# A two-layer streaming encoder: spatial mixing for eight feature tiles at once, first parts for the down projections in mid-group, parked sums in two steps a group

## The chip, the cores and the metric

The kernel runs on one core of one Trainium2 chip. The metric is device time in microseconds from launch to end; lower is better. Engines are named as in the profile: PE (matmul) with its weight loads (PEld), DVE (vector), ACT (scalar and activation), POOL and SP (here they only issue DMAs; POOL also makes a few constants).

## The reference

Two layers over 256 positions of 2048 features, all in fp32. Layer 0 mixes tokens with a gMLP spatial gating unit, layer 1 with latent attention; each mixer is followed by a gated MLP with a causal width-3 convolution, and each sub-layer ends in a layer norm of `ALPHA * x + sublayer(x)`. The parts that the change touches:

```python
def gmlp_mixer(x, w_in, ln_g, ln_b, w_s, b_s, w_out):
    z = jax.nn.gelu(x @ w_in)                       # 2048 -> 2 x 6144
    u, v = jnp.split(z, 2, axis=-1)
    v = layer_norm(v, ln_g, ln_b)
    v = v.reshape(B, S // 128, 128, 8, 768)         # windows of 128 positions, 8 groups of features
    w = w_s * mask[None]                            # chunk-causal, 128 x 128 for each group
    s = jnp.einsum('gij,bnjgd->bnigd', w, v) + jnp.transpose(b_s)[None, None, :, :, None]
    return (u * s.reshape(B, S, HALF)) @ w_out      # 6144 -> 2048

def conv_ffn(x, w_up, conv_w, conv_b, w_down):
    h = conv(x @ w_up) + conv_b                     # 2048 -> 2 x 5504, causal, width 3, per feature
    a, g = jnp.split(h, 2, axis=-1)
    return (jax.nn.silu(g) * a) @ w_down            # 5504 -> 2048
```

## The kernel before

Every weight passes through the core once, in chunks of 128 x 2048 fp32 (1 MB). SP loads a chunk into one of three `raw` buffers. ACT casts it to a high part (`wh`, line 127), DVE subtracts to a low part (`wl`, line 130). A product is made of high times high, high times low and low times high, all through the helper `mm`, so nearly every matmul has line 234. `Feed` keeps the order of the chunks: `feed.next()` hands out the next one, and casts and loads some chunks ahead, into 14 slots of one size with the tag `big`. Those slots also hold the activations. A second tag, `side`, has six slots.

Order: first the v half of the gMLP (six slices), then the u half, then the gMLP's down projection ("wo"), the first gated MLP ("up", then "dn"), attention, and the second gated MLP. A scheduler orders the instructions of each engine from the program order, its own estimates, and the order that is fixed by `keep_in_program_order` (`pin`).

The u half has 12 groups (`gi`) of four feature tiles. A group accumulates four PSUM banks over four chunks, in a wide pass (moving 512 columns) and a narrow one (256) for each chunk; the order of the two alternates, so that a group begins and ends with 16 wide matmuls. Eight banks exist in the pool. After a group, `gate` treats its tiles one after the other: ACT copies one half of the bank (`lo_u`, line 388), DVE adds the other (`h_u`, line 390), ACT applies GELU (line 788), PE mixes positions with the group's 128 x 128 weights (`s`: two matmuls a tile, two records each), DVE makes a bias (`sb`, line 793), scales the mixed values (`sg`, line 798, two operations of 128 columns) and multiplies (`pT`, line 800).

An up projection has 21 groups of up to four banks (two tiles of `a`, two of `g`). Group 1 to 20 have four chunks, group 21 has two. After a group, `pair` runs the convolutions and the gate on ACT and DVE (lines 388, 390, 835 to 853).

Some down chunks are of the kind "seven": beside the parts of the weights they need parts of sums of weights. For eight chunks per gated MLP these parts are made during the up projection and parked in HBM ("parked"; `park`, lines 150 to 181). A piece goes in steps: POOL's queue loads the chunk (`praw`, line 164); ACT casts, DVE subtracts, POOL stores two parts (`pwh`, `pwl`); DVE makes four additions in place (line 154); ACT casts, DVE subtracts, POOL stores the parts of the sums (`pth`, `ptl`). `next(jobs, None)` runs one step, behind every chunk from group 2 on; the steps of a piece are six, two of them empty. Later the parts are fetched back from HBM to the `side` slots.

`acts.make` makes the high and low parts of the activations of one unit (two tiles) of a down projection: unit 0 and 2 of "dn" are wide (a cast and a low part), unit 1 is parked and needs four subtractions (`turn`, lines 290 to 293) and two casts with their low parts. Units 0 and 1 are made after group 19, unit 2 after group 20.

The places in the code that set this order:

```python
for f in range(4): gate(4 * gi + f, acc[f])        # u half, after each group
if gi > 1: next(jobs, None)                        # up projection, behind each chunk
if gi == 19: acts.make(units 0 and 1)              # up projection, after the group
if gi == 20: acts.make(unit 2)
```

Of the kernel before, what the change touches and what calls it, by code (L numbers as in the profile page):

```python
# [15 lines left out]
P = 128  # L16
S = 256
# [43 lines left out]
        NF_FF: ("0e 1p 2e 3s 4e 5e 6p 7e 8s 9e 10e 11p 12e 13s 14e 15p 16e 17s 18e 19s 20e 21e",  # L61
                "21e 20e 19p 18e 17s 16e 15p 14e 13s 12e 11p 10s 9e 8s 7p 6e 5s 4e 3e 2e 1e 0e")}
KINDS = {"e": "wide", "s": "seven", "p": "parked"}
LEAD = 5
KEEP = {"wide": 4, "seven": 6, "parked": 6}

# [6 lines left out]
class Feed:  # L73
# [76 lines left out]
    def park(self, i):  # L150

        nc, pin = self.nc, self.pin
        tile = lambda n, dt: self.pool.tile([P, 2048], dt, tag="side", name=f"{n}{i}", bufs=SLOTS["side"])
        add = lambda o, a, b: pin(nc.vector.tensor_tensor(o, a, b, ALU.add))
        self.kept[i] = kept = {}

        def store(n, t, cols):
            d = self.dram.tile([P, cols], F32, tag=f"kept{n}{i}", name=f"kept{n}{i}", bufs=1)
            pin(nc.gpsimd.dma_start(d, t[:, 0:cols].bitcast(F32)))
            kept[n] = d  # L160

        ap = self.chunks[i][0]
        raw = tile("praw", F32)
        pin(nc.gpsimd.dma_start(raw.rearrange("p (k c) -> p k c", k=ap.shape[1]), ap))
        yield
        yield
        yield
        for n, o, cols in (("w", 512, 1536), ("t", 0, 2048)):
            hi, lo = tile(f"p{n}h", F32R), tile(f"p{n}l", F32R)
            pin(nc.scalar.copy(hi[:, 0:cols], raw[:, o : o + cols]))  # L170
            pin(nc.vector.tensor_tensor(lo[:, 0:cols], raw[:, o : o + cols], hi[:, 0:cols].bitcast(F32), ALU.subtract))  # L171
            store(f"{n}h", hi, cols)
            store(f"{n}l", lo, cols)
            if n == "w":
                yield
                r = [raw[:, 512 * i : 512 * (i + 1)] for i in range(4)]
                add(r[1], r[1], r[0])
                add(r[0], r[0], r[2])
                add(r[2], r[2], r[1])
                add(r[3], r[3], r[2])  # L180
                yield
# [32 lines left out]
def trunk(ctx: ExitStack, tc: tile.TileContext, x, xT, gm_in, gm_wout, ffn_up, ffn_dn,  # L214
# [12 lines left out]
    def slot(shape, name, dt=F32, tag="big"):  # L227
        return big.tile(shape, dt, tag=tag, name=name, bufs=SLOTS[tag])

    def bank(name):  # L230
        return ps.tile([P, 512], F32, tag="bank", name=name)
# [154 lines left out]
    def sum_halves(acc, name):  # L386
        lo = tp.tile([P, S], F32, tag="t1", name=f"lo_{name}", bufs=T1)
        nc.scalar.copy(lo, acc[:, S : 2 * S])
        h = tp.tile([P, S], F32, tag="t1", name=f"h_{name}", bufs=T1)
        nc.vector.tensor_tensor(h, acc[:, 0:S], lo, ALU.add)  # L390
        return h
# [90 lines left out]
    def down(n_k, src, tag, ln, acts, skew=SKEW):  # L482

        ln.begin()
        seq = plan(n_k)
        line = seq[0] + seq[1]
        late, at = [], 0
        fetched = max([i for i, t in enumerate(line) if t[1] == "parked"], default=len(line))
        for hf, units in enumerate(seq):
            n = len(units)  # L490
            last = [u for u, kind in units if kind != "wide"][-1]
            acc = Banks(f"{tag}{hf}", OWN + DIRECT if hf else DIRECT + OWN)
            for i, (u, kind) in enumerate(units):
                left = n - 1 - i if hf == 1 else n
                for n2, v2 in enumerate(line[at : at + 3]):
                    acts.make(*v2, "side" if at + n2 > fetched or at + n2 >= len(seq[0]) and v2[1] == "parked" else "big")
                if i == n - 8:
                    ln.fetch(hf)
                got = feed.next(splits=2 if left > 5 or left == 0 else 3, loads=2 if left > 2 or left == 0 else 1)
                if left == 6:  # L500
                    ln.prep()
                a, sums = acts.got[u]
                if left < skew:
                    late.append((a, *got))
                elif kind == "wide":
                    acc.eight(a, *got)
                else:
                    acc.seven(a, sums, *got, 512 if kind == "parked" else 0)
                    if u == last:
                        for j, t in enumerate(acc.rest()):  # L510
                            ln.fold(j // 2, 2 * hf + j % 2, t)
                at += 1
                for v2 in [v2 for v2 in acts.got if not any(v2 == w2 and n2 < KEEP[kind2]
                                                            for n2, (w2, kind2) in enumerate(line[at:]))]:
                    acts.got.pop(v2)
            if hf == 0:
                for j, m in enumerate(DIRECT):
                    ln.piece(j // 2, j % 2, acc.acc[m])

        def end(b, f):  # L520
            for i, (a, hi, lo) in enumerate(late):
                for j in range(len(a[b])):
                    prod_b([acc.acc[DIRECT[2 * b + f - 2]]], a[b][j], hi, lo, [(j * 1024 + (f - 2) * 512, 512)],
                           False, i == len(late) - 1 and j == len(a[b]) - 1)

        return [[None, None] + [acc.acc[DIRECT[2 * b + f]] for f in range(2)] for b in range(2)], end
# [251 lines left out]
    pT = [None] * 6  # L778
    acts = Acts(pT, "wo", NF_GM)

    def gate(F, acc):
        g = F // 6
        sl, pos = F // 8, F % 8
        if pT[sl] is None:
            pT[sl] = slot([P, 8, S], f"pT{sl}", tag="side" if sl else "big")
        h = sum_halves(acc, f"u{F}")
        u = tp.tile([P, S], F32, tag="t1", name=f"u{F}", bufs=T1)
        nc.scalar.activation(u, h, AF.Gelu_apprx_tanh)
        sp = bank(f"s{F}")
        for b in range(2):  # L790
            mm(sp[:, b * P : (b + 1) * P], v[sl][:, b, pos * P : (pos + 1) * P], wTg[:, g, :], True, True)
        t = tp.tile([P, P], F32, tag="sbias", name=f"sb{F}", bufs=1)
        nc.vector.scalar_tensor_tensor(t, rowsum[:, g, :], cst[:, C_GMB + F : C_GMB + F + 1], bsb[:, g, :],
                                       ALU.mult, ALU.add)
        s = tp.tile([P, S], F32, tag="t1", name=f"sg{F}", bufs=T1)
        for b in range(2):
            c = slice(b * P, (b + 1) * P)
            nc.vector.scalar_tensor_tensor(s[:, c], sp[:, c], cst[:, C_GMG + F : C_GMG + F + 1], t,
                                           ALU.mult, ALU.add)
        nc.vector.tensor_tensor(pT[sl][:, pos, :], u, s, ALU.mult)  # L800

    def park_all(until):

# [5 lines left out]
    for gi in range(12):  # L809
        acc = [bank(f"u{gi}_{f}") for f in range(4)]  # L810
        for c in range(4):
            hi, lo = feed.next()
            prod_a(acc, xhl, range(4 * c, 4 * c + 4), hi, lo)
            if gi > 0:
                next(jobs, None)
            if gi % 2 == 0 and gi < 10 and c in (1, 2):
                norm_v(gi // 2 + 1, c - 1)
        if gi == 11:
            for t in plan(NF_GM)[0][:2]:
                acts.make(*t)  # L820
        for f in range(4):
            gate(4 * gi + f, acc[f])
        if gi == 10:
            acts.make(*plan(NF_GM)[0][2])

# [16 lines left out]
    def ffn(layer, ln, acc, end, last):  # L842
# [28 lines left out]
        for gi in range(1, 22):  # L871
            nt, nk = (4, 4) if gi < 21 else (2, 8)
            acc = [bank(f"up{layer}_{gi}_{f}") for f in range(nt)]
            for c in range(KD // nk):
                hi, lo = feed.next()
                prod_a(acc, xhl, range(nk * c, nk * c + nk), hi, lo)
                if gi > 1:
                    next(jobs, None)
                if gi == 1 and c == 0:
                    after(1, 1, None)  # L880
                    for f in range(2):
                        pair(f, hb[0][:, f * S : (f + 1) * S], hb[1][:, f * S : (f + 1) * S])
            for f in range(nt // 2):
                pair(2 * gi + f, acc[f], acc[nt // 2 + f])
            if 1 < gi < 6:
                old.restore(gi - 2)
            if gi in (4, 6):
                old.park(gi // 2 - 2)
            if gi == 19:
                for t in plan(NF_FF)[0][:2]:  # L890
                    acts.make(*t)
            if gi == 20:
                acts.make(*plan(NF_FF)[0][2])
        ln = Norm(2 * layer + 1, {}, old.put_away, last)
        return (ln, *down(NF_FF, act, f"dn{layer}", ln, acts, 4 if last else SKEW))

# [379 lines left out]
```

## Time and profile before

| | |
|---|---|
| runs shown | 2482.6, 2479.5, 2482.21 us |
| median | 2482.21 us |
| the profiled execution | 2481.38 us |
| its span, first to last instruction | 2479.3 us |
| granted TensorE clock | 0.999 |
| u half of the gMLP, on PE | from 256.2 us to 547 us |
| first up projection | from 821 us to 1283 us |
| second up projection | from 1789 us to 2247 us |

All times inside an execution are microseconds from the start of the span. A row of a timeline has the start, the length, the engine, the line, the operation, the tiles written and read, the shape, the count of instructions merged in it and, in brackets, the idle time before it with what ended that. A row of the groups has the count, busy us, mean ns of one, and the idle time before them by what ended it. A row of the waits has who waited for whom, then us in total, times and the longest. Matmuls are pipelined, so the length of one is more than the distance to the next. A stall of PE is therefore read from the starts.

### The profile page before, as it was taken

What the parts mean: (1) busy time and instruction counts of PE and PEld (TensorE: products, weight loads), DVE (VectorE), ACT (ScalarE), POOL (GpSimd) and SP (SyncE); (2) the same over time, 40 slices, a digit from 0 to 9 for tenths busy, and PEclk for the clock granted to TensorE, in tenths of its full rate; (3) what the DMA queues carried; (4) which work ended last, traced back from release to release, by engine and by line L of the source; (5) the groups of instructions that cost most, each with busy time, mean ns of one, the idle gap of its engine ahead of it and who ended that gap; (6) DMA issues with size and microseconds to landing.
All of it is one profiled execution on the core that took longest, in us unless ns stands there. A gap on an engine that the chain in (4) does not pass through costs nothing. (4 is left out here: it accounts for less than half of the span.)

```text
span 2479.3 us, 33472 instructions
## 1 busy us (share of the span) xinstructions
PE 2463.7 (99%) x12947; PEld 2117.2 (85%) x12947; DVE 1999.7 (81%) x2834; ACT 1428.6 (58%) x1995; POOL 88.4 (4%) x171
## 2 busy tenths in 40 slices
PE   9999999999999999999999999999999999999998
PEld 7888888888888888888888888988888888888886
DVE  7999866679898788787677897867598778768798
ACT  6666544456565756566554466565566656555453
POOL 0000000000000000000000000000000000000000
PEclk9999999999999999999999999999999999999999
DMA  7556544556665689788558885544488789647885
GB/s 280 204 206 220 202 170 170 182 175 216 209 204 204 216 349 342 298 323 325 182 199 327 301 295 191 189 157 161 171 307 331 292 331 352 233 153 287 298 326 201
DMA packets 108992, 606.16 MB, mean 244 GB/s; under 512 B 10273, under 2 KB 11041, under 8 KB 61601
## 3 DMA queue, kind: packets, MB, share of 16 engines
q1 hardware_dynamic: 84832, 463.51, 52.6%
q0 software_dynamic: 24000, 140.52, 14.8%
q8 instruction: 101, 1.65, 0.3%
q14 instruction: 59, 0.48, 0.1%
HBM read 538.98 MB, written 65.01 MB: 244 GB/s over the span
## 5 line engine op out<-in xcount | busy, mean ns | idle before, releaser
L130 DVE TENSOR_TENSOR wl<-raw,wh 128x1024 fp32r<-128x1024 f32 (+4 forms) x693 | 968.7, 1419 | 214.2 <-ACT wh L127 130.7
L127 ACT CAST wh<-raw 128x1024 fp32r<-128x1024 f32 (+4 forms) x693 | 820.3, 1211 | 387.5 <-PE u L234 84.6
L234 PE MATMUL up<-xhl,wh 128*128 128x512 f32 x2624 | 612.0, 390 | 0.9 <-ACT wh L127 0.9
L234 PEld LDWEIGHTS up<-xhl,wh 128*128 128x128 f32 x2624 | 487.2, 188 | 99.5 <-ACT wh L127 1.8
L234 PEld LDWEIGHTS up<-xhl,wl 128*128 128x128 f32 x2624 | 325.9, 192 | 8.4 <-DVE wl L130 2.1
L234 PE MATMUL up<-xhl,wl 128*128 128x256 f32 x2624 | 328.9, 283 | 1.4 <-DVE wl L130 1.4
L234 PE MATMUL u<-xhl,wh 128*128 128x512 f32 x768 | 184.7, 393 | 0.1
L234 PEld LDWEIGHTS u<-xhl,wh 128*128 128x128 f32 x768 | 141.1, 188 | 31.5 <-issue 3.7
L127 ACT CAST th<-ts 128x1536 fp32r<-128x1536 f32 x106 | 110.1, 1051 | 85.1 <-DVE ts L137 59.4
L130 DVE TENSOR_TENSOR tl<-ts,th 128x1536 fp32r<-128x1536 f32 x106 | 125.4, 1218 | 8.0 <-PE dn_p L234 3.4
L234 PEld LDWEIGHTS u<-xhl,wl 128*128 128x128 f32 x768 | 95.5, 192 | 1.9
L234 PE MATMUL u<-xhl,wl 128*128 128x256 f32 x768 | 96.0, 283 | 0.0
L234 PE MATMUL mo<-wh,oT 128*128 128x512 f32 x256 | 82.4, 401 | 0.0
L137 DVE TENSOR_TENSOR ts<-ts,raw 128x512 f32<-128x512 f32 x106 | 72.7, 686 | 0.9
L234 PE MATMUL v_q<-wh,xhl 128*128 128x512 f32 x224 | 69.3, 390 | 1.0 <-ACT wh L127 1.0
L137 DVE TENSOR_TENSOR ts<-raw 128x1024 f32<-128x1024 f32 x53 | 64.6, 1218 | 0.9 <-PE wo_q L234 0.7
L234 PE MATMUL v_p<-wh,xhl 128*128 128x512 f32 x192 | 59.8, 390 | 0.1
L234 PEld LDWEIGHTS mo<-wh,oT 128*128 128x128 f32 x256 | 45.5, 189 | 7.1
L234 PEld LDWEIGHTS v_q<-wh,xhl 128*128 128x128 f32 x224 | 42.0, 188 | 10.7 <-ACT wh L127 2.2
L234 PE MATMUL mo<-wl,oT 128*128 128x512 f32 x128 | 50.0, 390 | 0.0
L171 DVE TENSOR_TENSOR pwl<-praw,pwh 128x1536 fp32r<-128x1536 f32 x16 | 28.1, 1756 | 26.1 <-ACT pwh L170 26.1
L683 ACT ACTIVATE lny<-lnt,lncol 128x128 f32<-128x128 f32 x96 | 36.6, 471 | 15.7 <-PE lnt L679 15.5
(1703 smaller groups left out, 4169.1 us busy)
## 6 DMA issues: line engine op xcount, KB each, us to landing
raw<-in_ffn_up_dram SPq DMA_DIRECT2D x172, 1024.0 KB, 5.8
raw<-in_gm_in_dram SPq DMA_DIRECT2D x93, 1024.0 KB, 4.9
raw<-in_ffn_dn_dram SPq DMA_DIRECT2D x68, 1024.0 KB, 7.1
raw<-in_gm_wout_dram SPq DMA_DIRECT2D x48, 1024.0 KB, 5.4
praw<-in_ffn_dn_dram POOLq DMA_DIRECT2D x16, 1024.0 KB, 15.8
keptth<-pth POOLq DMA_DIRECT2D x16, 1024.0 KB, 6.5
kepttl<-ptl POOLq DMA_DIRECT2D x16, 1024.0 KB, 9.5
fth<-keptth POOLq DMA_DIRECT2D x16, 1024.0 KB, 9.9
```

The lines of the kernel that those rows point to most:

```text
L127: cast = self.nc.scalar.copy(hi, raw)
L130: self.nc.vector.tensor_tensor(lo, raw, hi.bitcast(F32), ALU.subtract)
L137: add = lambda o, a, b: self.nc.vector.tensor_tensor(o, a, b, ALU.add)
L171: pin(nc.vector.tensor_tensor(lo[:, 0:cols], raw[:, o : o + cols], hi[:, 0:cols].bitcast(F32), ALU.subtract))
L234: recent[0] = nc.tensor.matmul(o, l, r, start=start, stop=stop, skip_group_check=True)
L683: nc.scalar.activation(y[:, j], t[:, j * P : (j + 1) * P], AF.Identity, bias=lncol[:, o : o + 1], scale=lncol[:, g : g + 1])
```

## The change

It has three parts.

1. `gate` is replaced by `spatial` and `scaled`. After each even group PE mixes the positions of eight tiles (this group's and the next's) into four banks, two tiles to a bank. The four copies and sums come first, then four GELUs in place. After an even group DVE makes for each of the eight tiles the bias and one mixing operation of 256 columns, straight into `pT`. After every group four products follow, in place in `pT`. After an odd group there is no mixing.
2. A unit's first parts for "dn" are made inside the groups: unit 0 behind the second chunk of group 19, unit 1 behind the first chunk of group 20, unit 2 behind its third. (The new condition `v2[0] < 20` in `down` changes nothing with these plans: no parked unit has a number of 20 or more.)
3. `park` loses its two empty steps, so that a piece has four. A step runs only behind the second and the third chunk of a group, from the third chunk of group 2 on.

```diff
+FIRST = ((19, 1), (20, 0), (20, 2))
...
         pin(nc.gpsimd.dma_start(raw.rearrange("p (k c) -> p k c", k=ap.shape[1]), ap))
-        yield
-        yield
         yield
...
-                    acts.make(*v2, "side" if at + n2 > fetched or at + n2 >= len(seq[0]) and v2[1] == "parked" else "big")
+                    acts.make(*v2, "side" if at + n2 > fetched or at + n2 >= len(seq[0]) and v2[1] == "parked" and v2[0] < 20 else "big")
...
-    def gate(F, acc):
-        g = F // 6
-        sl, pos = F // 8, F % 8
...
-        h = sum_halves(acc, f"u{F}")
-        u = tp.tile([P, S], F32, tag="t1", name=f"u{F}", bufs=T1)
-        nc.scalar.activation(u, h, AF.Gelu_apprx_tanh)
-        sp = bank(f"s{F}")
-        for b in range(2):
-            mm(sp[:, b * P : (b + 1) * P], v[sl][:, b, pos * P : (pos + 1) * P], wTg[:, g, :], True, True)
...
-        for b in range(2):
-            c = slice(b * P, (b + 1) * P)
-            nc.vector.scalar_tensor_tensor(s[:, c], sp[:, c], cst[:, C_GMG + F : C_GMG + F + 1], t,
-                                           ALU.mult, ALU.add)
-        nc.vector.tensor_tensor(pT[sl][:, pos, :], u, s, ALU.mult)
+    def spatial(sl):
+
+        pT[sl] = slot([P, 8, S], f"pT{sl}", tag="side" if sl else "big")
+        sp = [bank(f"s{sl}_{i}") for i in range(4)]
+        for pos in range(8):
+            for b in range(2):
+                o = (pos % 2) * S + b * P
+                mm(sp[pos // 2][:, o : o + P], v[sl][:, b, pos * P : (pos + 1) * P], wTg[:, (8 * sl + pos) // 6, :],
+                   True, True)
+        return sp
+
+    def scaled(sl, sp):
+        for pos in range(8):
+            F = 8 * sl + pos
+            t = tp.tile([P, P], F32, tag="sbias", name=f"sb{F}", bufs=1)
+            nc.vector.scalar_tensor_tensor(t, rowsum[:, F // 6, :], cst[:, C_GMB + F : C_GMB + F + 1],
+                                           bsb[:, F // 6, :], ALU.mult, ALU.add)
+            nc.vector.scalar_tensor_tensor(pT[sl][:, pos, :].rearrange("p (b c) -> p b c", b=2),
+                                           sp[pos // 2][:, pos % 2 * S : pos % 2 * S + S].rearrange("p (b c) -> p b c", b=2),
+                                           cst[:, C_GMG + F : C_GMG + F + 1], t[:, None, :].to_broadcast([P, 2, P]),
                                            ALU.mult, ALU.add)
...
-        for f in range(4):
-            gate(4 * gi + f, acc[f])
+        if gi % 2 == 0:
+            sp = spatial(gi // 2)
+        hs = [sum_halves(acc[f], f"u{4 * gi + f}") for f in range(4)]
+        for h in hs:
+            nc.scalar.activation(h, h, AF.Gelu_apprx_tanh)
+        if gi % 2 == 0:
+            scaled(gi // 2, sp)
+        for f, h in enumerate(hs):
+            t = pT[gi // 2][:, 4 * (gi % 2) + f, :]
+            nc.vector.tensor_tensor(t, t, h, ALU.mult)
...
-                if gi > 1:
+                if gi > 1 and c in (1, 2) and gi + c > 3:
                     next(jobs, None)
+                if (gi, c) in FIRST:
+                    acts.make(*plan(NF_FF)[0][FIRST.index((gi, c))])
...
-            if gi == 19:
-                for t in plan(NF_FF)[0][:2]:
-                    acts.make(*t)
-            if gi == 20:
-                acts.make(*plan(NF_FF)[0][2])
```

More of the change, by code (lines that the diff above doesn't have):

```diff
@@ L779, in trunk @@
     acts = Acts(pT, "wo", NF_GM)
-    def gate(F, acc):
-        g = F // 6
-        sl, pos = F // 8, F % 8
-        if pT[sl] is None:
-            pT[sl] = slot([P, 8, S], f"pT{sl}", tag="side" if sl else "big")
-        h = sum_halves(acc, f"u{F}")
-        u = tp.tile([P, S], F32, tag="t1", name=f"u{F}", bufs=T1)
-        nc.scalar.activation(u, h, AF.Gelu_apprx_tanh)
-        sp = bank(f"s{F}")
-        for b in range(2):
-            mm(sp[:, b * P : (b + 1) * P], v[sl][:, b, pos * P : (pos + 1) * P], wTg[:, g, :], True, True)
-        t = tp.tile([P, P], F32, tag="sbias", name=f"sb{F}", bufs=1)
-        nc.vector.scalar_tensor_tensor(t, rowsum[:, g, :], cst[:, C_GMB + F : C_GMB + F + 1], bsb[:, g, :],
-                                       ALU.mult, ALU.add)
-        s = tp.tile([P, S], F32, tag="t1", name=f"sg{F}", bufs=T1)
-        for b in range(2):
-            c = slice(b * P, (b + 1) * P)
-            nc.vector.scalar_tensor_tensor(s[:, c], sp[:, c], cst[:, C_GMG + F : C_GMG + F + 1], t,
+    def spatial(sl):
[16 more added lines that the diff above has]
+                                           cst[:, C_GMG + F : C_GMG + F + 1], t[:, None, :].to_broadcast([P, 2, P]),
                                            ALU.mult, ALU.add)
-        nc.vector.tensor_tensor(pT[sl][:, pos, :], u, s, ALU.mult)
     def park_all(until):
```

## The prediction

> **What bounds the kernel now.** I read the page first (span, busy shares), then the waits of PE and of its weight loads, and then PE's timeline over the two stages that the change touches.
>
> ```profile
> span 2479.3 us, 33472 instructions
> PE 2463.7 (99%) x12947; PEld 2117.2 (85%) x12947; DVE 1999.7 (81%) x2834; ACT 1428.6 (58%) x1995; POOL 88.4 (4%) x171
> ```
>
> PE works nearly all the time. The change removes no matmul, so it can gain only where PE now starts a matmul later than its pace allows. DVE, at 81%, is the engine nearest behind it. The waits of the weight loads, from 280 to 560 us, name the places of the u stage (us in total, times, longest):
>
> ```profile
> PEld u L234 <- issue: 3.7, 9, 0.4
> PEld wo_q L234 <- DVE h_u L390: 0.3, 1, 0.3
> ```
>
> Nine waits in eleven group changes, and one at the entry to the gMLP down projection. Matmul lengths overlap, so I measure a wait by the distance between starts in PE's timeline (start, length, then the group):
>
> ```profile
> 302.92 1.95 PE L234 MATMUL s<-wT,v 128*128 128x128 f32 x16
> 304.62 4.16 PE L234 MATMUL u<-xhl,wh 128*128 128x512 f32 x16
> 308.62 4.00 PE L234 MATMUL u<-xhl,wl 128*128 128x256 f32 x32
> 312.45 7.44 PE L234 MATMUL u<-xhl,wh 128*128 128x512 f32 x32
> 319.74 4.00 PE L234 MATMUL u<-xhl,wl 128*128 128x256 f32 x32
> ...
> 523.32 3.91 PE L234 MATMUL u<-xhl,wh 128*128 128x512 f32 x16
> 527.08 4.00 PE L234 MATMUL u<-xhl,wl 128*128 128x256 f32 x32
> ...
> 545.68 1.95 PE L234 MATMUL s<-wT,v 128*128 128x128 f32 x16
> 547.69 0.72 PE L234 MATMUL wo_q<-wh,wo0wx 128*128 128x512 f32 x2
> ```
>
> The pace: 32 wide matmuls take 7.29 us (312.45 to 319.74, 0.228 each), 32 narrow ones 3.83 (308.62 to 312.45). After spatial mixing the first 16 wide ones take 4.00 us at 304.62, but 3.76 at 523.32, where nothing waited: 0.24 us lost per waiting group change. The last spatial block needs 2.01 us to the next start, the one at 302.92 only 1.70: 0.31 lost at the entry to wo. The two up projections lose time in four places:
>
> ```profile
> 1256.93 3.82 PE L234 MATMUL up<-xhl,wh 128*128 128x512 f32 x16
> 1261.21 3.93 PE L234 MATMUL up<-xhl,wh 128*128 128x512 f32 x16 [0.47 <-ACT wh L127]
> 1264.97 1.24 PE L234 MATMUL up<-xhl,wl 128*128 128x256 f32 x9
> ...
> 1980.93 3.03 PE L234 MATMUL up<-xhl,wl 128*128 128x256 f32 x24
> ...
> 1985.19 5.18 PE L234 MATMUL up<-xhl,wh 128*128 128x512 f32 x22
> ...
> 2014.70 2.07 PE L234 MATMUL up<-xhl,wl 128*128 128x256 f32 x16
> 2017.52 1.22 PE L234 MATMUL up<-xhl,wl 128*128 128x256 f32 x8 [0.75 <-DVE wl L130]
> 2019.26 1.21 PE L234 MATMUL up<-xhl,wl 128*128 128x256 f32 x8 [0.52 <-DVE wl L130]
> 2020.31 4.04 PE L234 MATMUL up<-xhl,wh 128*128 128x512 f32 x17
> ...
> 2224.63 3.94 PE L234 MATMUL up<-xhl,wh 128*128 128x512 f32 x16 [0.47 <-ACT wh L127]
> ```
>
> At 1261 the 32 wide matmuls took 8.04 us for 7.29: 0.75 lost; 2224.63 is the same place of the second layer with the same 0.47 of idleness, 0.75 again. At 1984 32 narrow ones took 4.26 for 3.83 (0.43 lost), at 2014.70 5.61 (1.78 lost). The first layer's parking shows no such row.
>
> **The change part by part.**
>
> *Spatial mixing for eight tiles.* The same 192 records run, now as six blocks of 32 behind the even groups, none behind the odd ones. The wait is one for PSUM banks: the kernel's pool has eight, four hold the group, four the mixing, and the next group needs four that are free. The sums that free the group's banks come late, because each stands behind the GELU and the mixing of the tile before it:
>
> ```profile
> 302.50 0.37 ACT L388 COPY lo_u<-u 128x256 f32<-128x256 f32 x1 [2.96 <-PE u L234]
> 303.12 1.05 ACT L127 CAST wh<-raw 128x1024 fp32r<-128x1024 f32 x1 [0.25 <-PE u L234]
> 304.39 0.35 ACT L388 COPY lo_u<-u 128x256 f32<-128x256 f32 x1
> ...
> 302.90 0.42 DVE L390 TENSOR_TENSOR h_u<-u,lo_u 128x256 f32<-128x256 f32 x1 [1.01 <-ACT lo_u L388]
> 304.78 0.42 DVE L390 TENSOR_TENSOR h_u<-u,lo_u 128x256 f32<-128x256 f32 x1 [0.60 <-ACT lo_u L388]
> 308.07 0.41 DVE L390 TENSOR_TENSOR h_u<-u,lo_u 128x256 f32<-128x256 f32 x1
> ```
>
> The last sum starts at 308.07, over 5 us after the group ended. After the change an odd group (five of the nine waits) leaves four banks free from the start: 5 x 0.24 = 1.2 us gained. Behind an even group the block lasts twice 1.70 = 3.4 us, to 306.3, and the four copies and sums come first: 302.50 + 4 x 0.37 + two casts of 1.05 + 0.42 = 306.5 for the last sum, whose bank the fourth matmul wants at about 307.0. So the other four waits go too, 1.0 us. Bounds for those: 1.0 gained, or, if the four GELUs of 0.41 still come in between, a last sum at 308.1 and 1.1 us lost at each of six blocks, 6.6 lost. I take the gain, since the copies are now issued ahead of the GELUs. Wo's entry follows an odd group with four banks free: 0.31 gained (bounds 0 and 0.31).
>
> What hides the rest is PE's lead over DVE. These groups price the DVE work (busy us, mean ns):
>
> ```profile
> L130 DVE TENSOR_TENSOR wl<-raw,wh 128x1024 fp32r<-128x1024 f32 x516 | 615.5, 1219 | 140.6 <-ACT wh L127 82.4 <-issue 52.0 <-PE u L234 4.1
> L798 DVE SCALAR_TENSOR_TENSOR sg<-s,cst,sb 128x128 f32<-128x128 f32 x96 | 29.1, 344 | 4.5 <-PE s L234 2.4
> L838 DVE SCALAR_TENSOR_TENSOR c_1g<-h_1g,cst,c_1g 128x254 f32<-128x254 f32 x41 | 19.7, 480 | 0.7
> L793 DVE SCALAR_TENSOR_TENSOR sb<-rsum,cst,wT 128x128 f32<-128x128 f32 x48 | 16.5, 344 | 0.0
> ```
>
> Two mixing operations of 344 ns become one over 256 elements. No row shows it; between one of them (344) and two (688) I take 480, the same operation over 254. That takes some 48 x 0.2 = 10 us off DVE, none of it on the path. But the work comes in one lump behind each even group: four sums (1.7), eight bias and mixing pairs (8 x 0.82 = 6.6), four products (1.7): 10 us. A low part (two of 1.22) queued behind it is ready at 12.4 us; PE wants the third chunk's low half at 3.4 + 5.55 x 2 + 3.65 = 18 us. Cost taken: nothing. Without that lead it would be the second rival below. [...]
>
> *First parts in mid-group.*
>
> ```profile
> 1259.59 0.62 ACT L473 CAST dn01px<-dn01pt 128x512 fp32r<-128x512 f32 x1 [1.29 <-DVE dn01pt L290]
> ```
>
> ACT sits 1.29 us behind the convolutions until it may cast unit 1's sums, and the weight cast that PE wants at 1260.56 is queued behind it. Unit 1 (four DVE subtractions, two casts, two low parts) moves behind the next group's first chunk, whose weight casts are issued in front of it; units 0 and 2 (a cast and a low part each) move half a group earlier. Gain 2 x 0.75 = 1.5 us. Unit 0's buffer takes one of the 14 big slots some two chunks sooner, which leaves five for pairs of weight parts, still more than two chunks: taken at nothing, at worst the 1.5 stays. None of these steps issues a DMA.
>
> *Parked sums.* Each of 16 pieces keeps one load and four stores on POOL's queue, two casts on ACT, six operations on DVE. Two empty steps go; four steps per piece run at two per group, so a piece takes 8 chunks (44 us) where it took 6 (33 us), and parking ends in group 18, not 14. Load to first cast stays three chunks, the load stays one chunk behind the last step of the piece before; the additions now finish three chunks ahead of that last step, not one, and no step is issued at a group's change, where the convolutions run. The losses at 1984 and 2014 come from here:
>
> ```profile
> 1987.71 0.53 POOL L159 DMA_DIRECT2D kepttl<-ptl  x1 [2.00 <-DVE ptl L171]
> 1988.25 0.71 POOL L164 DMA_DIRECT2D praw<-in_ffn_dn_dram  x1
> 2005.99 1.48 ACT L170 CAST pwh<-praw 128x1536 fp32r<-128x1536 f32 x1 [3.53 <-DMA praw<-in_ffn_dn_dram]
> ```
>
> The load waits on POOL behind the store of the late low part, lands late, ACT stands 3.53 us, and the weight casts behind it come late. With the additions done earlier the store and the load go out sooner. SP, which loads the chunks, is not passed. Gain 0.43 + 1.78 = 2.2; bounds 2.2 and, the first layer having parked without loss and four more groups now parking, a loss of another 2.2.
>
> Where DMAs meet, these stretches of two groups show it (with parking, without; DMA share and GB/s last):
>
> ```profile
> 1969.10:2013.50 44.40, 44.23 (x255) 39.02 (x254) 32.99 (x48) 25.79 (x37) 3.39 (x6) 1.00 0.73 279
> 1180.00:1224.40 44.40, 44.40 (x257) 39.31 (x257) 29.74 (x44) 24.11 (x37) 0.00 (x0) 1.00 0.55 190
> ```
>
> The share is far from full, so I expect longer but thinner parking to help. [...]
>
> **The sum.** 1.2 + 1.0 + 0.3 + 1.5 + 2.2 = 6.2 us off the profiled execution of 2481.4 (span 2479.3, 2.1 around it) gives 2475.2. The median of the runs is 0.8 above the profiled one, so I predict 2476.0.
>
> **The rivals.**
>
> *Parking costs PE the same.* The load still trails the last low part on POOL, and ACT still stands for it. For: that order of issue is kept. Against: the earlier additions. Gain 4.0: 2478.2, no change that can be told.
>
> *The lump on DVE slows it.* If a low part for the odd group's second chunk is queued behind the lump, it is ready at 12.4 us where PE wants it at 3.4 + 5.55 = 9.0: 3.4 us at six blocks is 20, so 2482.2 - 4.0 + 20 = 2498. It decides from 1.5 us a block on. For: DVE's work behind an even group is never so long now. Against: DVE idled 1.01 us before the sum at 302.90, so that low part was done.
>
> *The moved first parts don't help*, the casts keeping their place in ACT's order or the slot being missed: gain 4.7, 2477.5.
>
> **How the numbers follow.** A measurement of this kernel tells about 0.2% (5 us) from no change, so faster means below 2477.2, slower above 2487.2. Chances: forecast 0.60 (own range 2474 to 2477.2), parking unchanged 0.18, first parts of no help 0.10, DVE's lump 0.12. That is faster 0.60, same 0.28, slower 0.12. The range starts at 2473, the fastest run before (2479.5) less 6.2, and reaches to 2484, the forecast with the bank bound at its worst (2476.0 + 1.0 + 6.6 = 2483.6), over both middle rivals; the DVE case stays out.
>
> **What would show it.** Right: no waits of weight loads for issue in the u stage, even blocks of 32 records followed at once by 16 wide matmuls in about 3.76 us, no idle time ended by the high parts near the end of either up projection, none by the low parts in group 9 to 11 of the second. Wrong: PE waiting for a low part in an odd u group, for sums behind a block, or for weights in groups 14 to 18.

## The result and the profile after

The changed kernel takes 2474.44 us (median of 11 runs, 2474.23 to 2475.92), the kernel before 2481.15 in the same comparison (11 runs, 2479.0 to 2484.11). The ratio is 0.9974, 95% interval 0.9964 to 0.9983: faster by 0.26%. The runs also lie closer together, 1.7 us apart where they were 5.1 apart. The profiled execution took 2475.22 us with a span of 2473.0.

The page of the changed kernel, and ACT's waits for the parked loads, first before the change and then after it:

```profile
span 2473.0 us, 33399 instructions
PE 2460.1 (99%) x12947; PEld 2118.2 (86%) x12947; DVE 1992.8 (81%) x2786; ACT 1425.3 (58%) x1995; POOL 88.3 (4%) x171
```

```profile
ACT pwh L170 <- DMA praw<-in_ffn_dn_dram: 34.3, 10, 6.0
```

```profile
ACT pwh L169 <- DMA praw<-in_ffn_dn_dram: 3.6, 2, 2.1
```

The count of PE's instructions is the same, DVE has 48 fewer (one mixing operation for two), and ACT's waits for parked loads went from ten (34.3 us) to two (3.6 us).

From the starts of the first matmuls in the two timelines the stages last (us):

| from, to | before | after | difference |
|---|---|---|---|
| u half: first `u` to first `wo_q` | 291.54 | 288.67 | -2.87 |
| gMLP down projection, to first `upf` | 253.25 | 253.10 | -0.15 |
| first up projection, first `up` to first `dn_q` | 462.30 | 461.49 | -0.81 |
| attention layer, from the first `mq` up to the second `upf` | 256.18 | 256.25 | +0.07 |
| second up projection, first `upf` to first `dn_q` | 484.73 | 481.66 | -3.07 |
| second down projection, to PE's last matmul | 221.45 | 221.90 | +0.45 |

These add up to 6.4 us less; the spans differ by 6.3. PE's timeline after, at the places that the prediction showed:

```profile
326.90 3.73 PE L233 MATMUL s<-wT,v 128*128 128x128 f32 x32
330.39 3.89 PE L233 MATMUL u<-xhl,wh 128*128 128x512 f32 x16
334.11 4.00 PE L233 MATMUL u<-xhl,wl 128*128 128x256 f32 x32
...
541.22 3.82 PE L233 MATMUL u<-xhl,wh 128*128 128x512 f32 x16
544.87 0.62 PE L233 MATMUL wo_q<-wh,wo0wx 128*128 128x512 f32 x2
...
1253.92 7.44 PE L233 MATMUL up<-xhl,wh 128*128 128x512 f32 x32
1261.20 4.00 PE L233 MATMUL up<-xhl,wl 128*128 128x256 f32 x32
...
2010.48 4.00 PE L233 MATMUL up<-xhl,wl 128*128 128x256 f32 x32
2014.32 7.44 PE L233 MATMUL up<-xhl,wh 128*128 128x512 f32 x32
```

The block of 32 records is followed at once by 16 wide matmuls in 3.72 us (330.39 to 334.11), where it was 4.00. Wo starts 3.65 us after the last 16 wide ones began, which is their pace. The 32 wide matmuls of the former loss at 1261 take 7.28 us, not 8.04, and the 32 narrow ones of the former loss at 2014 take 3.84, not 5.61.

### The profile page after: what moved, and what is told of

The parts are those of the page before. It is cut to its first block, busy times and chain, and to the rows that moved or that the text cites. A ratio compares the mean times of both kernels' runs of the same rounds, so it can differ in the third digit from the quotient of the medians.

```text
span 2473.0 us, 33399 instructions
## 1 busy us (share of the span) xinstructions
PE 2460.1 (99%) x12947; PEld 2118.2 (86%) x12947; DVE 1992.8 (81%) x2786; ACT 1425.3 (58%) x1995; POOL 88.3 (4%) x171
## 3 DMA queue, kind: packets, MB, share of 16 engines
q8 instruction: 101, 1.65, 0.3%
## 5 line engine op out<-in xcount | busy, mean ns | idle before, releaser
L155 DVE TENSOR_TENSOR praw<-praw 128x512 f32<-128x512 f32 x64 | 43.9, 686 | 0.6
```

## The experiments

### Each part alone

The first three kernels are the kernel before with one part of the diff each, the fourth changes only how many banks the mixing holds. The first:

```diff
-        for f in range(4):
-            gate(4 * gi + f, acc[f])
+        if gi % 2 == 0:
+            sp = spatial(gi // 2)
+        hs = [sum_halves(acc[f], f"u{4 * gi + f}") for f in range(4)]
...
```

> The change's first part alone (spatial mixing for eight tiles, copies and sums first) on the kernel before. Theory of the prediction: the group changes of the u half lose their waits and nothing else moves: the u half takes 288.7 us instead of 291.5 (2.9 less), both up projections keep their losses near 1260 and 2224, and the time is 2.9 us (0.11%) below the kernel before. Rival, that the smaller load on DVE helps elsewhere too: the up projections get faster as well, more than 4 us in all.

Measured: u half 288.67 us (2.87 less), as in the whole change. The first up projection keeps its loss (462.25). The median is 2479.9 against 2480.95, ratio 0.9996 (0.9987 to 1.0006): about 1 us, but the interval takes in both the 2.9 us and no change at all. In its profile the second up projection took 464.90 from first `up` to first `dn_q`, where the profile before has 464.46: the losses at the old steps are still there. The theory's place and size hold in the u half, and the rival's faster up projections don't show. Whether anything else moved, these runs don't tell.

```diff
+                if (gi, c) in FIRST:
+                    acts.make(*plan(NF_FF)[0][FIRST.index((gi, c))])
...
-            if gi == 19:
-                for t in plan(NF_FF)[0][:2]:
-                    acts.make(*t)
-            if gi == 20:
-                acts.make(*plan(NF_FF)[0][2])
```

> The second part alone (units 0, 1 and 2 made in mid-group). Theory: the weight cast that stood behind unit 1's cast comes in time; each up projection loses the 0.75 us near its end and nothing else: 1.5 us (0.06%) below the kernel before. Rival, that the wait comes from the number of big slots and not from ACT's order: the earlier unit 0 makes it no better, 0 to 1 us slower.

Measured: first up projection 461.50 (0.80 less), u half unchanged (291.42). Median 2479.18, ratio 0.999 (0.9981 to 1.0). The second up projection of the profiled execution, the slowest of its ten, took 465.36: the losses at the old steps were larger there. That execution comes back below.

```diff
-        yield
-        yield
         yield
...
-                if gi > 1:
+                if gi > 1 and c in (1, 2) and gi + c > 3:
                     next(jobs, None)
```

> The third part alone (four steps a piece, two a group). Theory: the first up projection is unchanged but for its 0.75 us near the end, the second loses its 0.43 and 1.78: 2.2 us (0.09%) below the kernel before in a profile, and the runs lie closer together than before's. Rival, parking costs PE the same wherever its steps stand: the losses only move into groups 9 to 18, no change.

Measured: first up projection 462.26, second 462.22, so the two losses of 0.43 and 1.78 are gone and the 0.75 near the end stays in both. The ten runs lie within 1.65 us (2479.2 to 2480.85), where the 31 runs of the kernel before spread over 6.6 in that comparison (2478.77 to 2485.34). The median is 2479.76 against 2480.95, ratio 0.9995 (0.9985 to 1.0004). So the third part takes off the runs' upper end. The best runs of the kernel before lie below this kernel's best, so they can have had hardly any of that loss.

```diff
+    def mixed(gi):
+        sps = [bank(f"s{gi}_{i}") for i in range(2)]
+        for F in range(4 * gi, 4 * gi + 4):
+            for b in range(2):
+                o = F % 2 * S + b * P
+                mm(sps[F % 4 // 2][:, o : o + P], v[F // 8][:, b, F % 8 * P : (F % 8 + 1) * P], wTg[:, F // 6, :], True, True)
+        return sps
...
-        sp = bank(f"s{F}")
-        for b in range(2):
-            mm(sp[:, b * P : (b + 1) * P], v[sl][:, b, pos * P : (pos + 1) * P], wTg[:, g, :], True, True)
+        sp = sps[F % 4 // 2][:, F % 2 * S : F % 2 * S + S]
```

> The kernel before with one edit: the spatial mixing of a group's four tiles is issued at once, two tiles to a PSUM bank, so that it holds two banks and not four; copies, sums, GELUs and the mixing on DVE stay one tile after the other and per group. Theory, the nine waits are for banks: two more free banks end them, the u half is 9 x 0.24 = 2.2 us shorter (289.3). Rival, the waits end because the copies and sums come first: this kernel keeps them, u half 291.5.

Measured: u half 289.37 us, 2.17 less; median 2479.08 against 2480.95, ratio 0.9989 (0.9979 to 0.9999). Its timelines of PE and DVE at the group change, PE's at the entry to wo, and the waits of its weight loads from 280 to 560 us:

```profile
302.92 1.95 PE L234 MATMUL s<-wT,v 128*128 128x128 f32 x16
304.62 3.96 PE L234 MATMUL u<-xhl,wh 128*128 128x512 f32 x16
308.41 4.00 PE L234 MATMUL u<-xhl,wl 128*128 128x256 f32 x32
...
543.84 1.95 PE L234 MATMUL s<-wT,v 128*128 128x128 f32 x16
545.54 0.71 PE L234 MATMUL wo_q<-wh,wo0wx 128*128 128x512 f32 x2
```

```profile
304.77 0.42 DVE L390 TENSOR_TENSOR h_u<-u,lo_u 128x256 f32<-128x256 f32 x1 [0.15 <-ACT lo_u L388]
306.35 0.41 DVE L390 TENSOR_TENSOR h_u<-u,lo_u 128x256 f32<-128x256 f32 x1
308.00 0.41 DVE L390 TENSOR_TENSOR h_u<-u,lo_u 128x256 f32<-128x256 f32 x1
```

```profile
PEld u L234 <- issue: 1.7, 9, 0.2
```

The sums come as late as before (the last at 308.00, against 308.07), and still the 16 wide matmuls need 3.79 us, not 4.00. Wo starts 1.70 us after the last mixing block began, not 2.01. So the 2.17 us are some 0.2 us at each of nine group changes and 0.3 at the entry to wo. The waits were for banks, and the rival falls: the sums didn't have to come earlier. Two more banks don't end the waits altogether: the weight loads still wait nine times for issue, 1.7 us in all where it was 3.7, and the 16 wide matmuls need 3.72 us in the changed kernel.

### Do the sums have to come first?

The changed kernel with copy, sum, GELU, mixing and product of one tile after the other:

```diff
-        hs = [sum_halves(acc[f], f"u{4 * gi + f}") for f in range(4)]
-        for h in hs:
-            nc.scalar.activation(h, h, AF.Gelu_apprx_tanh)
...
+        for f in range(4):
+            h = sum_halves(acc[f], f"u{4 * gi + f}")
+            nc.scalar.activation(h, h, AF.Gelu_apprx_tanh)
+            if gi % 2 == 0:
+                scaled(gi // 2, sp, 2 * f, 2 * f + 2)
+            t = pT[gi // 2][:, 4 * (gi % 2) + f, :]
+            nc.vector.tensor_tensor(t, t, h, ALU.mult)
```

> The changed kernel with copy, sum and GELU done one tile after the other, each followed by its share of the mixing and its product, instead of all copies and sums first; the mixing matmuls of eight tiles stay together. Theory of the prediction, behind an even group the last sum must come before PE wants its bank: 0.2 to 1.1 us lost at each of up to six blocks, u half 290 to 295. Rival, the free banks decide alone and the longer block of 3.5 us covers late sums: u half 288.7.

Measured: u half 288.68 us, the same as the changed kernel's 288.67 (one run, 2474.72 us). The prediction's bound falls, and the rival holds in its number. DVE and PE behind an even group:

```profile
330.74 0.41 DVE L389 TENSOR_TENSOR h_u<-u,lo_u 128x256 f32<-128x256 f32 x1
```

```profile
326.81 3.73 PE L233 MATMUL s<-wT,v 128*128 128x128 f32 x32
330.30 3.89 PE L233 MATMUL u<-xhl,wh 128*128 128x512 f32 x16
334.02 4.00 PE L233 MATMUL u<-xhl,wl 128*128 128x256 f32 x32
```

The last sum ends at 331.15, 0.85 us after PE went on, and 16 wide matmuls still take 3.72 us. The fourth of them, the first into the fourth accumulator, starts at 331.07, before that sum ends. So PE wanted other banks than the one that the last sum frees.

### Which first part was it?

The kernel before with unit 1 alone moved:

```diff
             if gi == 19:
-                for t in plan(NF_FF)[0][:2]:
-                    acts.make(*t)
+                acts.make(*plan(NF_FF)[0][0])
...
+                if (gi, c) == (20, 0):
+                    acts.make(*plan(NF_FF)[0][1])
```

> The kernel before with unit 1's first parts alone moved behind the first chunk of group 20; units 0 and 2 where they were. Theory, the wait near 1260 comes from unit 1's cast standing in front of the weight cast on ACT: both up projections lose their 0.75 us (first up projection 461.5). Rival, it takes the earlier unit 0 as well, since its low part too stands in that queue on DVE: 0.3 to 0.75 us of the wait stay.

Measured, in one run of 2479.5 us: first up projection 461.49 us, the whole 0.8 less. PE's timeline there:

```profile
1258.38 7.44 PE L234 MATMUL up<-xhl,wh 128*128 128x512 f32 x32
1265.67 2.56 PE L234 MATMUL up<-xhl,wl 128*128 128x256 f32 x20
```

The 32 wide matmuls take 7.29 us: no wait. Unit 1's place behind the chunk's weight casts is the whole effect: the kernel with all three units moved has 461.50. The second up projection takes 461.80 here, so this execution, with the old steps of the parked sums, lost only some 0.35 us at them.

### What was it about the parked sums?

Six kernels, all of them the changed one with other steps. The first three keep four steps and eight chunks a piece, with other places:

```diff
-                if gi > 1 and c in (1, 2) and gi + c > 3:
+                if (4 * gi + c) % 8 in (0, 3, 4, 7) and 4 * gi + c > 11:
                     next(jobs, None)
```

> The changed kernel with the parked sums' steps behind the fourth and first chunk of a group instead of the second and third: the same four steps a piece, the same distances between them, two a group, all of it half a group later. Theory A, the place in the group counts (casts of parked pieces must stay away from the convolutions at a group's change): ACT waits for the loads again or the weight casts come late, the second up projection loses 1 to 3 us and the runs spread over more than 3 us. Theory B, the thinner and wider schedule counts: both up projections stay at 461.5, no difference, spread under 2 us.

Measured: 2474.8 us (2474.42 to 2476.68), up projections 461.50 and 461.45, and ACT never waits for a parked load. The place in the group does not count.

```diff
-                if gi > 1 and c in (1, 2) and gi + c > 3:
+                if (4 * gi + c) % 8 in (2, 5, 6, 7) and 4 * gi + c > 9:
                     next(jobs, None)
```

> The changed kernel with a piece's last step one chunk behind its additions, as before the change, and not three; a piece still takes eight chunks, and its successor's load then comes three chunks behind that last step and not one. Theory A, what helped is the distance from the additions to the casts of the sums: the last low part comes late again, waits for it in the second up projection return, 1 to 3 us. Theory B, what helped is that the load no longer goes out late behind that low part, or the lower rate: here the load has more room still, ACT's wait for it is 0 to 4 us in all, and the up projections stay at 461.5.

Measured: 2474.66 us (2474.4 to 2476.14), up projections 461.53 and 461.47, and again no wait of ACT for a load. The distance from the additions to the last casts does not count by itself. Here the next load has room; the next kernel takes that away too:

```diff
-                if gi > 1 and c in (1, 2) and gi + c > 3:
+                if (4 * gi + c) % 8 in (0, 1, 2, 5) and 4 * gi + c > 9:
                     next(jobs, None)
```

> The changed kernel, a piece still taking eight chunks, but its last three steps as close as before the change: additions one chunk ahead of the last step, the next load one chunk behind it, the first cast three chunks behind the load; the spare chunks stand between the first cast and the additions. Theory A, the chain of late low part, late load and ACT waiting for the load is what costs PE, and distances alone cure it: ACT's wait for the loads comes back (over 15 us in all), the up projections lose 1 to 3 us. Theory B, the rate alone counts (eight chunks instead of six for the same work): ACT's wait under 6 us, up projections 461.5.

Measured: 2474.88 us (2474.53 to 2476.09), up projections 461.49 and 461.46, ACT's wait for loads 8.2 us in four, less than theory A expected and more than theory B. With the old tight distances but eight chunks a piece nothing is lost. Theory A in the form "distances alone" falls. The next kernel undoes the third part:

```diff
-                if gi > 1 and c in (1, 2) and gi + c > 3:
+                if gi > 1:
                     next(jobs, None)
...
         yield
+        yield
+        yield
```

> The changed kernel with the third part undone: six steps a piece, one behind every chunk. Both theories: ACT waits over 30 us for the loads, the second up projection loses 1 to 3 us, runs spread over more than 3 us, median 1 to 3 us above the changed kernel's.

Measured: 2478.18 us, ten runs from 2474.61 to 2480.0; first up projection 461.53, second 465.33; ACT's wait for the loads 32.3 us in nine. The loss is back, 3.3 us in the median above the kernel just shown, which was compared with it (2474.88). PE's timeline at one place of it, then ACT's and DVE's:

```profile
2010.34 2.07 PE L235 MATMUL up<-xhl,wl 128*128 128x256 f32 x16
2013.33 1.21 PE L235 MATMUL up<-xhl,wl 128*128 128x256 f32 x8 [0.92 <-DVE wl L131]
```

```profile
2001.81 1.47 ACT L171 CAST pwh<-praw 128x1536 fp32r<-128x1536 f32 x1 [5.13 <-DMA praw<-in_ffn_dn_dram]
2003.18 0.60 ACT L845 ACTIVATE c_1a<-h_1a,cst 128x256 f32<-128x256 f32 x1
...
2009.04 1.98 ACT L128 CAST wh<-raw 128x1024 fp32r<-128x1024 f32 x2
```

```profile
2003.82 0.48 DVE L846 SCALAR_TENSOR_TENSOR c_1a<-h_1a,cst,c_1a 128x255 f32<-128x255 f32 x1 [4.97 <-ACT c_1a L845]
...
2010.01 2.14 DVE L155 TENSOR_TENSOR praw<-praw 128x512 f32<-128x512 f32 x3
2012.06 1.22 DVE L131 TENSOR_TENSOR wl<-raw,wh 128x1024 fp32r<-128x1024 f32 x1
```

ACT stands 5.13 us for the parked load. The convolution behind it is late, so DVE idles 4.97 us and then has it all to do. When the weight cast that PE needs comes (2009.04), three parked additions (2.14 us) stand on DVE ahead of its low part. Two kernels take away one of the two halves each. The next piece's load ahead of the last step, with rate and work as before:

```diff
-        ap = self.chunks[i][0]
-        raw = tile("praw", F32)
-        pin(nc.gpsimd.dma_start(raw.rearrange("p (k c) -> p k c", k=ap.shape[1]), ap))
+        if first:
+            load(i)
+        raw = self.ahead_raw
...
                 add(r[3], r[3], r[2])
+                if after is not None:
+                    load(after)
```

> The old steps (six a piece, one behind every chunk) in the changed kernel, with the next piece's load issued behind the additions, ahead of the last step, so that it no longer trails the late low part; rate and work unchanged. Theory A (late load): ACT's wait for the loads falls from over 30 us to under 8, and the losses of the up projections go, spread under 2 us. Theory B (rate): the losses stay, 1 to 3 us, though ACT does not wait for the loads.

Measured: 2474.88 us (2474.33 to 2476.07), up projections 461.49 and 461.44. POOL's timeline of this kernel shows the load ahead of the store of the sums' high part, some 23 us ahead of the store of the last low part, behind which it stood:

```profile
1958.44 0.53 POOL L160 DMA_DIRECT2D keptwl<-pwl  x1 [1.26 <-DVE pwl L177]
1958.96 0.71 POOL L166 DMA_DIRECT2D praw<-in_ffn_dn_dram  x1
1979.30 0.55 POOL L160 DMA_DIRECT2D keptth<-pth  x1 [19.62 <-ACT pth L176]
1981.82 0.53 POOL L160 DMA_DIRECT2D kepttl<-ptl  x1 [1.97 <-DVE ptl L177]
```

ACT's wait for the loads is gone altogether, and so is PE's loss, at the old rate. And the old steps without the additions (the parked sums are then plain weights):

```diff
-                add(r[1], r[1], r[0])
-                add(r[0], r[0], r[2])
-                add(r[2], r[2], r[1])
-                add(r[3], r[3], r[2])
```

> The old steps in the changed kernel with the four additions of every parked piece left out, so that the parked sums are plain weights and the output is not the reference's; DMAs, casts and low parts as they were. Theory B read as DVE's load: 2.7 us of DVE less a piece ends the losses. Theory B read as DMA traffic: the traffic is the same and the losses stay, 1 to 3 us. Theory A: the low part is earlier, so the load is; losses mostly gone, ACT's wait for the loads halved at least.

Measured: up projections 461.47 and 461.46, no loss, though ACT's wait for the loads is as long as ever:

```profile
ACT pwh L171 <- DMA praw<-in_ffn_dn_dram: 35.1, 10, 5.2
```

That contradicts the expectation that the loads would come earlier, and the reading by DMA traffic, which was unchanged. So the loss needs both: ACT held by a late load, and parked additions on DVE in front of the weights that come late for it. With either half taken away, PE lost nothing in the profiled execution.

Both together don't always cost PE time. These are ACT's waits for the loads in the kernel before, in the first and in the second up projection:

```profile
ACT pwh L170 <- DMA praw<-in_ffn_dn_dram: 16.0, 5, 4.2
```

```profile
ACT pwh L170 <- DMA praw<-in_ffn_dn_dram: 18.3, 5, 6.0
```

They are nearly the same, with the same additions, and only the second up projection loses time by them. Against 461.45 us, and without the 0.75 near the end, the second one lost 0.35 us (unit 1 alone moved) to 3.9 (third part undone; second part alone, there with about 1 us of it lost at half the clock, shown at the end) in the six profiled executions with the old steps and the additions. What decides how much is open.

The median without additions is 2475.73, 2.45 below the kernel with the third part undone and 0.85 above the kernel with the early load. In its profile 0.95 us more lie behind the start of PE's last matmul (11.80 us to the end, against 10.85), which no run explains.

## Why the prediction was right

The predicted 2476.0 stands 1.6 us above the measured 2474.44, inside the range. The 1.6 us are not in the sum: the prediction put the median 0.8 above the profiled execution, as before the change, and it came out 0.8 below (2474.44 against 2475.22). The sum, 6.2 us off the profiled execution, measured 6.3 between the spans. That it is so close is partly luck, since terms that were too small and a loss that was left out nearly cancel, and the parked sums' loss varies. Term by term:

*Odd and even group changes and wo's entry, 2.5 us.* Measured 2.87. The nine waits and the one at wo's entry are shown to be for banks by the kernel with two tiles to a bank, which took off 2.17 with the sums as late as before: some 0.2 of each 0.24, and the 0.3 at wo. The other 0.7 (289.37 to 288.67) came with the new blocks: two groups take 48.04 us from one block to the next, where two groups of that kernel take 48.20. One step was wrong: "the copies and sums come first", and the bound of 6.6 us lost if they did not. With one tile after the other the u half takes 288.68. I had priced the last sum against the bank of a fourth matmul at a fixed time. But that kernel's fourth matmul started before the last sum ended, and in the kernel before the scheduler had already put the matmuls off that would wait. The merged timeline row hides it, since the four accumulators share a name there. The first 16 wide matmuls behind nine of the mixing blocks before, and behind every block after, in the order in which the built kernels issue them:

```
before:  u0 u1 u2 u0 u1 u2 u0 u1 u3 u3 u2 u3 u0 u1 u2 u3
after:   u0 u1 u2 u3 u0 u1 u2 u3 u0 u1 u2 u3 u0 u1 u2 u3
```

In the kernel before, the last sum ended at 308.48, 3.9 us after PE went on at 304.62, and the group change lost 0.24 us.

*DVE's lump, taken at nothing.* Right: no wait in an odd u group (from 280 to 560 us no engine's work holds up a matmul or a weight load). The unseen operation that I priced at 480 ns from the convolution's row has its own row now, in the timeline behind an even group:

```profile
327.99 0.48 DVE L797 SCALAR_TENSOR_TENSOR pT<-s,cst,sb 128x256 f32<-128x256 f32 x1 [0.36 <-PE s L233]
```

It is 0.48 us, so the row of the nearest operation was the right price for it.

*First parts, 1.5 us.* Measured 0.80 in the first up projection of the kernel with that part alone, and 0.75 of the second's 3.03 from first `up` to first `dn_q`, by the place of the former wait. The cause is shown: unit 1 alone moved gives the same. The rival "the moved first parts don't help" fell.

*Parked sums, 2.2 us.* The size came out for the profiled pair (0.43 and 1.78 gone), but that is luck in part, for it is not a constant: alone the part moved the median by 1.2 us, in the changed kernel its absence costs 3.3, and the profiled executions with the old steps lost from 0.35 to 3.9. And the step that explained it, "with the additions done earlier the store and the load go out sooner", was not the reason. The place in the group, the distance of the additions and the distance of the load can each be put back without loss while a piece takes eight chunks. What the runs showed is that the loss needs ACT's wait for a late load together with additions queued in front of weights; the slower rate brings ACT's wait from 34.3 us to 3.6 (8.2 with the tight steps). Whether the rate acts through ACT's wait alone or also by thinning DVE's work isn't settled: the two were not parted at eight chunks. The rival "parking costs PE the same" fell: at unchanged traffic per piece the early load ended the loss, and groups 14 to 18 show no wait (PE was busy for all of the 112 us from 2070 to 2182, and of the 113 us from 1105 to 1218).

*What the sum left out.* The second down projection lost 0.45 us in the profiled execution, where its weight loads wait for the first parts of units 3 and 1:

```profile
PEld dn_q L233 <- DVE dn13wx L476: 0.4, 1, 0.4
PEld dn_q L233 <- DVE dn11wx L476: 0.4, 2, 0.2
```

The stage was 221.45 to 221.51 in the kernel before and ten of the experiments, 221.55 and 221.83 in the two others; it comes and goes, and its cause is open. And the terms may not be independent: each part alone moved the median by 1.0, 1.8 and 1.2 us, 4.0 together, where the whole moved it by 6.7. That the old parking gave part of the other gains back would fit its varying loss, but the intervals of the three are as wide as these numbers, so it isn't shown.

## What to carry to other kernels

On a kernel whose PE is busy 99% of the time, measure the starts of PE against its own pace in a stretch without waits, name what each late start stood for, and sum those; the sum held to 0.1 us here, with some luck, while no run shows that the 6.9 us which DVE was busy for less bought anything. A merged timeline row can hide that the scheduler has already moved work around a wait, so price a late release by the time that PE lost, not by how late the release is. And when runs spread, look for a queue in which a load is issued behind a late store, and for an engine that stands waiting for that load while work that PE needs is queued behind it. Issuing the load ahead of that store cured here what a slower schedule also cured.

## What the runs showed of the hardware

In the profiled execution of the kernel with the second part alone, two parking waits of PE close together were followed by 3 us at a granted clock of 0.50, with 0.86 in the us before and 0.93 in the us after. PE's timeline and the windows (us, PE busy, weight loads, DVE, ACT, POOL, granted clock, DMA share, GB/s):

```profile
1981.34 2.07 PE L235 MATMUL up<-xhl,wl 128*128 128x256 f32 x16
1984.55 1.21 PE L235 MATMUL up<-xhl,wl 128*128 128x256 f32 x8 [1.14 <-DVE wl L131]
1986.28 1.74 PE L235 MATMUL up<-xhl,wl 128*128 128x256 f32 x8 [0.52 <-DVE wl L131]
1987.83 8.51 PE L235 MATMUL up<-xhl,wh 128*128 128x512 f32 x32
1996.18 4.00 PE L235 MATMUL up<-xhl,wl 128*128 128x256 f32 x32
```

```profile
1983.00:1987.00 4.00, 2.34 (x17) 1.93 (x16) 4.00 (x5) 3.06 (x4) 0.00 (x0) 0.97 0.37 158
1986.00:1987.00 1.00, 0.72 (x5) 0.72 (x6) 1.00 (x2) 1.00 (x2) 0.00 (x0) 0.86 0.00 0
1987.00:1990.00 3.00, 3.00 (x11) 2.52 (x11) 3.00 (x3) 1.92 (x3) 0.67 (x2) 0.50 0.94 281
1990.00:1991.00 1.00, 1.00 (x6) 0.84 (x5) 1.00 (x2) 0.00 (x0) 1.00 (x2) 0.93 0.82 246
```

PE was busy 2.34 of 4 us, and then the clock stood at 0.50 while the wide matmuls ran: 32 of them take 8.35 us for 7.29, about 1 us on top of the 2 us waited. This was seen in one execution only. Shorter waits were not followed by it: in the kernel before, with waits of 0.75 and 0.52 us, PE was busy 2.73 of the 4 us from 2016 to 2020, and the clock stood at 1.00 in each of the 8 us from 2016 to 2024. In the kernel with the third part undone, with 0.92 and 0.52, PE was busy 2.55 of the 4 us from 2012 to 2016, and the first four wide matmuls behind that took 1.09 us, about 0.23 from start to start as at full pace. Whether the slower runs of the kernel before come from such a stretch is not shown; its profiled execution has none, up to the start of PE's last matmul. Nor does a trace show what set the clock to 0.50: the longest idle stretch in the rows above is 1.14 us.
